# Seven products for eight in the recurrence's projections, with the partial results added in PSUM, and Down's weight sums made by accumulating DMAs

## The chip, the cores and the metric

The kernel runs on one core of one Trainium2 chip. The core has TensorE (PE in the profile: matrix products, results into PSUM), VectorE (DVE), ScalarE (ACT), GpSimd (POOL) and SyncE (SP, which here only issues DMAs). SBUF is the core's working memory, with 128 partitions; PSUM holds eight banks of 512 float32 columns for each partition. The metric is device time in microseconds, the median of some runs.

## The reference

A trunk of two layers over 1024 tokens of width 1024, batch 1. The first layer mixes tokens with a gated linear recurrence of 8 heads of width 128. Its input projection gives four parts, and these projections are what the change touches:

```
q, f, i, g = split(h @ w_in, 4)              # w_in: 1024 x 4096
fg = lb + (1 - lb) * sigmoid(f)
o  = hgrn2_chunkwise(silu(q), 1 - fg, i, log(fg))
o  = o * rsqrt(mean(o^2) + eps) * gnorm_w * silu(g)
mix = o @ w_out
```

`hgrn2_chunkwise` evaluates `S_t = diag(f_t) S_{t-1} + k_t v_t^T`, `o_t = S_t^T q_t`, with k = 1 - fg and v = i. The second layer uses sliding-window attention. After each mixer come a layer norm, a gated feed-forward block (Up: 1024 to 2 x 2816 columns, a causal convolution of width 3, a SiLU gate; Down: 2816 to 1024) and another layer norm. All of it is float32.

## The kernel before, in words

**Precision.** A float32 matrix is split into a high part (rounded to float32r by an ACT copy) and a low part (the rest, by a DVE subtraction). `mm3` (lines 193 to 197) multiplies with three matmuls: high x high, high x low, low x high.

**Residents.** `T` holds the turned activations (channels on partitions), high and low. `Y` is a row buffer of 32 KB a partition. `HL` holds six pairs of high and low weight pieces of 1024 columns.

**Recurrence.** For each head, `qf` computes the query and forget projections with weights as the fixed operand: two halves of 512 tokens, 8 pieces of the contraction, three matmuls each. `ig_block` (L739, L740) computes value and gate with the tokens fixed: 8 blocks of 128 tokens, 8 pieces, and per piece one matmul of 512 columns (high and low weights side by side) and one of 256. `recur` then runs the head's own chain on DVE, PE and ACT, in steps that a generator yields; the heads follow one another in one task, `all_heads`. `norm` normalises, and turns the result back into T, by way of Y for heads 0 to 6. Seven heads' products run beside the previous head's chain.

**Order.** In the recurrence the order on all five engines is written out: the class `Order` counts PE's time (`t`) and DVE's (`v`) as instructions are laid, and steps each generator whose due time has come at every `tick`; `finish` and loops that call `step` run a generator to its end at once. In the feed-forward part only PE's order is written out; the Tile framework orders the others. Each engine's queue runs in order: an instruction that waits holds up those behind it.

**Down's weights.** Down already works with seven products of half blocks for eight, and needs sums of its weight blocks. `slot_begin` (L1193 and around) loads pairs of weight rows into free rows of Y during the recurrence, lays four DVE subtractions each (L1209), 88 for both layers, and stores the sums to the DRAM tile `bsd`, from which `operands` (L562) loads them in Down.

**Up** works with seven products too: `collect` (L477 to L490) adds the products into SBUF on DVE and ACT, and the convolution (L496, L498) follows. Here nothing of that changes.

**The seam.** After the last head the output projection `out_pass` (L1299) and `out_part` use T; `out_proj` loads the residual x into Y (L330), adds the product to it (L351) and starts the layer norms. The second half of the projection's weights comes through `out_late` (rx tiles, L164).

Of the kernel before, what the change touches and what calls it, by code (L numbers as in the profile page):

```python
# [16 lines left out]
P = 128  # L17
S = 1024
# [89 lines left out]
def trunk(ctx: ExitStack, tc: tile.TileContext, a: dict, out: bass.AP):  # L108
# [14 lines left out]
    par = cp.tile([P, 17], F32, name="par")  # L123
# [5 lines left out]
    Y = cp.tile([P, 8, D], F32, name="Y")  # L129
# [7 lines left out]
    nc.gpsimd.dma_start(gd1, a["ln_mix_g"])  # L137
    bsd = [drp.tile([P, FF // 256, 2, D], F32, name=f"bsd{l}") for l in range(2)]
# [54 lines left out]
    def mm3(ps, st, mv, start, stop, n=512):  # L193
        nc.tensor.matmul(ps, st(0), mv(0), start=start, stop=False)  # L194
        nc.tensor.matmul(ps, st(0), mv(1), start=False, stop=False)  # L195
        nc.tensor.matmul(ps, st(1), mv(0), start=False, stop=stop)  # L196
        od.t += 3 * n / 2365.0
# [176 lines left out]
    class Up:  # L374
# [131 lines left out]
        def run(self, ready, down):  # L506
# [18 lines left out]
            self.weights(2)  # L525
            for fc in range(2):
# [11 lines left out]
    class Down:  # L538
# [25 lines left out]
        def operands(self, i, k):  # L564
# [10 lines left out]
            elif p == 5:  # L575
# [3 lines left out]
                tt(R[:, 0], R[:, 0], x[:, 0], op=add)  # L579
                x = R  # L580
            elif p == 6:
                self.block_a(x[:, 0], k, 0, 0)
                self.sum_b(R[:, 1], k, 2)
                tt(R[:, 0], R[:, 0], x[:, 0], op=sub)
                x = R
            elif p == 7:
                self.block_a(x[:, 0], k, 1, 1)
                self.sum_b(x[:, 1], k, 3)
                tt(x[:, 0], x[:, 0], R[:, 0], op=sub)
            elif p == 3:  # L590
                self.block_a(x[:, 0], k, 0, 1)
                self.block_b(x[:, 1], k, 1, 1)
                tt(x[:, 0], x[:, 0], R[:, 0], op=sub)
# [16 lines left out]
        def evacuate(self, p, tb, ps, ln):  # L610
            lo, hi = [Y[:, t, :].rearrange("p (h n) -> p h n", h=2) for t in (tb, tb + 4)]
            both = ps.unsqueeze(1).to_broadcast([P, 2, 512])
            if p == 1:
                for y in (lo, hi):
                    nc.vector.scalar_tensor_tensor(y, y, ALPHA, both, op0=ALU.mult, op1=ALU.add)
            elif p in (6, 7):
                tt(hi, hi, both, op=add)
            for y in {2: [lo[:, 0]], 5: [lo[:, 1], hi[:, 1]], 6: [lo[:, 1]], 3: [lo[:, 1]], 4: [hi[:, 0]]}.get(p, []):
                tt(y, y, ps, op=add)
# [58 lines left out]
    with tc.tile_pool(name="t", bufs=1, reuse_waits="tile") as raws, hgrn_pool as hp:  # L678
        raw_tail(raws)

        def ig_load(h, u):
            return load(lambda r: [(r.rearrange("p (k g c) -> p k g c", k=4, g=2)[:, :, g, :],
                                    w_iv[:, 4 * u:4 * u + 4, (2 + g) * D + h * P:(2 + g) * D + (h + 1) * P])
                                   for g in range(2)])

        def ig_split(raw, eng=None):
            return split_raw(raw, eng).rearrange("p h (k c) -> p h k c", k=4)

        def qf_load(h, g):
            c0 = g * D + h * P  # L690
            return load(lambda r: [(r.rearrange("p (k c) -> p k c", k=KC), w_iv[:, :, c0:c0 + P])])

        def qf_split(raw, eng=None):
            return split_raw(raw, eng).rearrange("p h (k c) -> p h k c", k=KC)

        VG = {-1: hp.tile([P, NB, 2, P], F32, name="VG", bufs=2)}
        values_in, soon, gated = [-1], [], {}

        def values(h, tb, ps):

            vg = VG[h][:, tb]
            nc.scalar.copy(vg, ps[:, 256:].rearrange("p (g c) -> p g c", g=2))
            yield 0.9
            nc.vector.tensor_tensor(vg, vg, ps[:, :256].rearrange("p (g c) -> p g c", g=2), op=ALU.add)
            od.vec(0.45)
            if tb == NB - 1:
                values_in[0] = h
            if tb % 2:
                G = VG[h][:, tb - 1:tb + 1, 1, :]
                sg = hp.tile([P, 2, P], F32, name="sg")  # L710
# [6 lines left out]
        def first_values(ps):  # L717

            pv = ps.rearrange("p (t g c) -> p t g c", t=2, g=2)
            vg = VG[0][:, :2]  # L720
# [957 lines left out]
```

## Time and profile before

| | us |
|---|---|
| median of 3 runs | 2129.36 (2128.87 to 2130.18) |
| span of the profiled execution | 2126.5 |
| PE busy | 2116.9 |
| DVE busy | 1765.4 |
| ACT busy | 926.4 |
| POOL busy | 132.7 |

The profiled execution's own whole time is not listed; the median lies 2.9 us above its span. In the profile a line such as `L1209 DVE TENSOR_TENSOR Y<-Y 128x512` names the line of the kernel, the engine, the operation, and the tiles written and read; then come the count, the busy time with the mean of one, and the engine's idle time before it with what ended it. Matmul durations overlap, so distances between starts are the better measure of TensorE.

### The profile page before, as it was taken

Reading aid. Unit: us, or ns where it says so; the run is one execution under the profiler, and the core shown is the slowest. Engines: PE = TensorE matmul, PEld = TensorE weight load, DVE = VectorE, ACT = ScalarE, POOL = GpSimd, SP = SyncE. Lnnn points to the kernel's source line nnn. Section 1 sums busy time; section 2 is a strip of 40 time slices with the busy share of each in tenths; the row PEclk is TensorE's granted clock in tenths of the full one; section 3 lists DMA queues with packets and bytes.
Section 4 is the critical chain, followed back from the end, with each engine's and each line's share of the span. In section 5 each row is a group of like instructions: output and inputs, shape, how many; then the busy total and the mean of one; then the engine's idle time right before and its main releaser. Section 6 shows DMA issues by size and latency. Waiting matters only on the chain.

```text
span 2126.5 us, 32114 instructions
## 1 busy us (share of the span) xinstructions
PE 2116.9 (100%) x12639; PEld 1776.7 (84%) x12639; DVE 1765.4 (83%) x2378; ACT 926.4 (44%) x1491; POOL 132.7 (6%) x150
## 2 busy tenths in 40 slices
PE   9999999999999999999999999999999999999998
PEld 8888888888888888888888888888888888888887
DVE  4777776677999999888977758969999999878986
ACT  4444444452444444444433356743544444444430
POOL 1000000001100000000001113321000000000002
PEclk9999999999999999999999999999999999999999
DMA  6655443205223222238854511042232222249662
GB/s 218 245 210 168 145 131 120 75 30 180 100 83 98 88 90 80 80 99 272 293 183 166 161 31 41 24 149 90 80 105 94 90 89 80 89 147 334 220 207 97
DMA packets 231566, 280.53 MB, mean 132 GB/s; under 512 B 30152, under 2 KB 160376, under 8 KB 228600
## 3 DMA queue, kind: packets, MB, share of 16 engines
q1 hardware_dynamic: 230464, 278.11, 39.4%
q8 instruction: 99, 1.62, 0.3%
q10 hardware_dynamic: 856, 0.37, 0.1%
q14 instruction: 51, 0.42, 0.1%
q0 software_dynamic: 96, 0.02, 0.0%
HBM read 215.51 MB, written 62.94 MB: 131 GB/s over the span
## 4 chain that ended last, share of the span: by engine, by line
PE 99%; DMA 0%; DVE 0%; SPq 0%; issue 0%; DVEq 0%; ACT 0%; ACTq 0%
PE psmm L194 17%; PE psmm L196 17%; PE psmm L195 17%; PE psax L194 10%; PE psax L195 10%; PE psax L196 10%; PE psmm L739 5%; PE psax L200 4%; PE psmm L740 3%; PE psmm L204 1%; PE psmm L200 1%; PE psax L1452 1%; PE psax L204 1%; PE psmm L1299 1%; PE psmm L777 0%; DMA raw<-in_hgrn_w_in_dram 0%
## 5 line engine op out<-in xcount | busy, mean ns | idle before, releaser
L194 PE MATMUL psmm<-T,HL 128*128 128x512 f32 x768 | 303.5, 395 | 0.0
L196 PE MATMUL psmm<-T,HL 128*128 128x512 f32 x768 | 299.4, 390 | 0.0
L195 PE MATMUL psmm<-T,HL 128*128 128x512 f32 x768 | 299.2, 390 | 0.0
L498 DVE SCALAR_TENSOR_TENSOR Y<-Y,cwt 128x1023 f32<-128x1023 f32 (+1 forms) x176 | 224.9, 1281 | 45.3 <-ACT Y L496 43.9
L221 ACT CAST HL<-rx 128x1024 fp32r<-128x1024 f32 (+1 forms) x151 | 150.7, 1007 | 174.4 <-PE psmm L195 30.4
L169 DVE TENSOR_TENSOR HL<-rx,HL 128x1024 fp32r<-128x1024 f32 (+1 forms) x151 | 178.3, 1187 | 16.5 <-ACT HL L221 16.2
L739 PE MATMUL psmm<-HL,T 128*128 128x512 f32 x496 | 176.8, 399 | 0.0
L196 PEld LDWEIGHTS psmm<-T,HL 128*128 128x128 f32 x768 | 144.2, 188 | 30.5
L194 PEld LDWEIGHTS psmm<-T,HL 128*128 128x128 f32 x768 | 144.3, 188 | 29.7 <-issue 0.4
L195 PEld LDWEIGHTS psmm<-T,HL 128*128 128x128 f32 x768 | 144.4, 188 | 28.8 <-issue 0.4
L496 ACT ACTIVATE Y<-Y,cwt 128x1024 f32<-128x1024 f32 x88 | 108.7, 1238 | 101.5 <-DVE Y L485 89.1
L740 PE MATMUL psmm<-HL,T 128*128 128x256 f32 x496 | 138.9, 280 | 0.0
L194 PE MATMUL psax<-T,HL 128*128 128x512 f32 x352 | 137.3, 390 | 0.0
L196 PE MATMUL psax<-T,HL 128*128 128x512 f32 x352 | 137.0, 389 | 0.0
L195 PE MATMUL psax<-T,HL 128*128 128x512 f32 x352 | 137.0, 389 | 0.0
L243 POOL TENSOR_TENSOR rs<-rs,nhalf 128x1 f32<-128x1 f32 x32 | 44.6, 1396 | 1287.0 <-DVE rs L242 1287.0
L739 PEld LDWEIGHTS psmm<-HL,T 128*128 128x128 f32 x496 | 93.1, 188 | 21.0
L740 PEld LDWEIGHTS psmm<-HL,T 128*128 128x128 f32 x496 | 93.7, 189 | 0.4
L221 ACT CAST HT<-rx 128x1024 fp32r<-128x1024 f32 (+1 forms) x37 | 35.5, 961 | 125.6 <-DVE rx L452 76.7
L169 DVE TENSOR_TENSOR HL<-raw,HL 128x1024 fp32r<-128x1024 f32 x51 | 62.0, 1217 | 21.4 <-ACT HL L176 20.2
L196 PEld LDWEIGHTS psax<-T,HL 128*128 128x128 f32 x352 | 66.1, 188 | 13.6
L195 PEld LDWEIGHTS psax<-T,HL 128*128 128x128 f32 x352 | 66.1, 188 | 13.6
(316 smaller groups left out, 5229.5 us busy)
## 6 DMA issues: line engine op xcount, KB each, us to landing
rx<-in_ffn_w_in_dram SPq DMA_DIRECT2D x136, 256.0 KB, 3.2
rx<-gd SPq DMA_DIRECT2D x118, 256.0 KB, 3.8
Y<-in_ffn_w_out_dram SPq DMA_DIRECT2D x44, 512.0 KB, 6.0
bsd<-Y SPq DMA_DIRECT2D x22, 1024.0 KB, 4.8
gd<-Y SPq DMA_DIRECT2D x44, 512.0 KB, 2.6
rx<-in_ffn_w_out_dram SPq DMA_DIRECT2D x54, 256.0 KB, 4.8
R<-bsd SPq DMA_DIRECT2D x44, 256.0 KB, 5.1
Y<-in_ffn_w_in_dram SPq DMA_DIRECT2D x40, 256.0 KB, 2.9
```

What stands on the lines that cost most here:

```text
L169: make = lambda e: e.tensor_tensor(lo, src, hi.bitcast(F32), op=ALU.subtract)
L194: nc.tensor.matmul(ps, st(0), mv(0), start=start, stop=False)
L195: nc.tensor.matmul(ps, st(0), mv(1), start=False, stop=False)
L196: nc.tensor.matmul(ps, st(1), mv(0), start=False, stop=stop)
L200: nc.tensor.matmul(ps, lhsT, rhs, start=start, stop=stop, **kw)
L204: nc.tensor.transpose(ps, src, ident)
L221: nc.scalar.copy(hi, src)
L243: nc.gpsimd.tensor_tensor(rs, rs, nhalf, op=ALU.pow)
L496: nc.scalar.activation(c, u, AF.Identity, bias=cwt[:, l, 3, ci:ci + 1], scale=cwt[:, l, 2, ci:ci + 1])
L498: nc.vector.scalar_tensor_tensor(c[:, sh:], u[:, :S - sh], cwt[:, l, 2 - sh, ci:ci + 1], c[:, sh:], op0=ALU.mult, op1=ALU.add)
L739: nc.tensor.matmul(ps, T[:, 0, kc, ts], w[:, :, kc % 4, :], start=kc == 0, stop=False)
L740: nc.tensor.matmul(ps[:, :256], T[:, 1, kc, ts], w[:, 0, kc % 4, :], start=False, stop=kc == KC - 1)
```

## The change

- **Units.** For heads 1 to 7 the four projections become two units a head: q with f, and i with g. Each is the product of a weight block matrix (2 x 2 blocks: contraction halves by the two parts) with T (2 x 2: contraction halves by token halves), computed with seven products of half size. Product p is 4 contraction pieces x 3 matmuls of 512 columns.
- **Sums of x.** The block sums of the turned x are made once at the start from a staging tile XS (which replaces Y there); three go to HL (`tx`), and one replaces a quarter of T once head 0's second token half has been projected.
- **Weights.** Each unit's blocks are summed on DVE and split (`prepare`, `cast`) into a tile WR, one unit ahead. WR takes the memory of XS.
- **Adding in PSUM.** Products 1, 6, 7 and 4 go on in one bank, 5 and 3 in another; ACT or DVE read the bank between the products that need a partial result.
- **Values** come out with channels on partitions and are turned by eight transposes (`turn_values`). Gates stay turned, and `norm` multiplies them in after its own transposes.
- **Y** is allocated after the recurrence; heads 0 to 5 go by a DRAM tile `yd` into WR's rows.
- **Down's sums** are made from DRAM to DRAM in Up: 16 plain DMAs from SP and 16 accumulating DMAs from POOL for each layer. Signs in Down's operands and evacuations follow.

```
-    Y = cp.tile([P, 8, D], F32, name="Y")
+    yd = drp.tile([P, 6, S], F32, name="yd")
...
+        def sum_blocks(self):
+            n = FF // 256
+            wb = self.w.rearrange("(r k p) (c n) -> r c p k n", r=2, k=n, c=2)
+            t1, t3, t4, t2 = [self.sums[:, :, i, j * 512:(j + 1) * 512] for i in range(2) for j in range(2)]
+            steps = [((t1, wb[0, 0]), (t3, wb[1, 1]), (t2, wb[1, 1]), (t4, wb[1, 0])),
+                     ((t1, wb[0, 1]), (t3, wb[0, 1])), ((t2, t1),), ((t4, t2),)]
+            for i, step in enumerate(steps):
+                for dst, src in step:
+                    for k0, k1 in ((0, 3), (3, 6), (6, 9), (9, n)):
+                        if i:
+                            nc.gpsimd.dma_start(dst[:, k0:k1], src[:, k0:k1], accum_op=add)
+                        else:
+                            nc.sync.dma_start(dst[:, k0:k1], src[:, k0:k1])
+                        yield
...
             for fc in range(2, NF):
                 if fc > 2:
                     self.weights(fc)
+                for _ in range(2):
+                    next(sums, None)
...
-            early = stash(2, idle[:, :S])
+            early = stash(2, qs if h else VT)
...
+        bank = lambda u, p: {1: banks[u % 2 * 2], 5: banks[3], 3: banks[3], 2: banks[1]}.get(p, banks[u % 2 * 2])
+        units = [(kind, h) for h in range(1, NH) for kind in "qv"]
...
+        def cast(u, p, src):
+            w = WR[0][:, row_of(u, p), :]
+            nc.scalar.copy(w[:, :512], src)
+            job(0.8, 0.69, lambda: low_part(w[:, 512:], src, w[:, :512], None), ("lo", u, p))
...
+            if stage == 0:
+                cast(u, 1, b11)
+                cast(u, 3, b22)
+                plus(1, b11, b12)
+                plus(3, b12, b22)
+                plus(2, b22, b11)
+            elif stage == 1:
+                need(("sum", u, 1))
+                cast(u, 5, b11)
...
+            for k in range(4):
+                mm3(ps, lambda j: w[:, 512 * j + P * k:512 * j + P * k + P], lambda j: moving(j, k),
+                    p in (1, 5, 2) and k == 0, k == 3, more=p in (6, 7, 4, 3))
+                od.tick()
+            collect(u, p, ps)
...
+                def sum22():
+                    tt(st["c"][:, 512:], st["c"][:, 512:], banks[3], op=add)
+                    od.vec(0.69)
+                    od.spawn(second(u, 1), 0.8)
...
+        def drive(cond):
+            n = 0
+            while not cond():
+                for t in sorted(od.chains, key=lambda k: k[0]):
+                    if t is not params:
+                        od.step(t)
+                    if cond():
+                        return
+                if jobs:
+                    lay_job()
...
+        def first_unit():
+            while ("x", 5, 3) not in done_jobs:
+                yield 0.2
+            staging.close()
+            pool = ring_pool.enter_context(tc.tile_pool(name="wr", bufs=1, reuse_waits="tile"))
+            WR.append(pool.tile([P, 8, 1024], F32R, name="WR"))
+            for stage in range(5):
+                prepare(0, stage)
+                yield 1.6
+            prepared.append(0)
...
+            drive(lambda: prepared)
+            last = len(units) - 1
+            stages = {1: 0, 5: 1, 7: 2, 2: 3, 4: 4}
+            for u in range(last + 1):
+                order = [(u, p) for p in ((1, 6, 5, 7, 2, 3) if u < last else (1, 6, 2, 7, 5, 4, 3))]
+                if u:
+                    order.insert(1, (u - 1, 4))
+                for v, p in order:
+                    product(v, p)
...
+            drive(lambda: values_done[0] == NH - 1)
+            drive(lambda: all(m[1] is None for m in late_moves))
...
             for tb in range(4, 6):
                 begun.append(ps[:, (tb - 4) * 512:(tb - 3) * 512])
                 out_part(begun[tb], us, tb, range(KC - 1))
-            od.finish(normed)
+            drive(lambda: 7 in turned)
...
+    Y = ctx.enter_context(tc.tile_pool(name="yp", bufs=1, reuse_waits="tile")).tile([P, 8, D], F32, name="Y")
```

More of the change, by code (lines that the diff above doesn't have):

```diff
@@ L689, in qf_load @@
[L689 to L702, printed above, removed]
+        tail["raw"] = [raws.tile([P, 1024], F32, name=f"raw{i}") for i in range(4)]
@@ new lines, in trunk, with flat, load4, column @@
+        soon, normed = [], []
+        def flat(t):
+            return t.rearrange("p c d -> p (c d)")
+        def load4(loads):
+            raw = tail["raw"][ring["raw"] % 4]
+            ring["raw"] += 1
+            for view, src in loads(raw):
+                nc.sync.dma_start(view, src)
+            return raw
+        def column(g, h):
+            c0 = g * D + h * P
+            return load4(lambda r: [(r.rearrange("p (k c) -> p k c", k=KC), w_iv[:, :, c0:c0 + P])])
+        jobs, done_jobs = [], set()
```

666 lines of the change are left out of this document (416 added, 250 removed).

## The prediction

> **What bounds the kernel now.** I read the page's shares and chain first, then who made TensorE wait, then the busy times of single stages, then single rows of TensorE and VectorE (DVE).
>
> ```profile
> span 2126.5 us, 32114 instructions
> PE 2116.9 (100%) x12639; PEld 1776.7 (84%) x12639; DVE 1765.4 (83%) x2378; ACT 926.4 (44%) x1491; POOL 132.7 (6%) x150
> PE 99%; DMA 0%; DVE 0%; SPq 0%; issue 0%; DVEq 0%; ACT 0%; ACTq 0%
> ```
>
> ```profile
> PE psmm L834 <- DVE Y L785: 1.0, 1, 1.0
> PE psmm L777 <- ACT HL L766: 0.4, 1, 0.4
> PE psmm L777 <- DVE HL L757: 0.3, 1, 0.3
> ```
>
> TensorE is the chain that ends last, nearly alone, and all its waits together are 1.7 us. So every TensorE microsecond removed is worth one, as long as no new wait appears, and every new wait costs itself. That is also the danger: the old order has no wait left to hide a new one behind. The next rows (span of the stretch, busy time and count by engine, granted clock, DMA) show six heads of the recurrence and a piece of the first Up.
>
> ```profile
> 106.00:426.00 320.00, 320.00 (x3294) 272.65 (x3293) 225.75 (x418) 143.37 (x324) 12.87 (x14) 1.00 0.42 141
> 690.00:740.00 50.00, 50.00 (x223) 41.40 (x221) 45.74 (x50) 22.85 (x26) 0.00 (x0) 1.00 0.29 94
> ```
>
> In the recurrence DVE is busy 225.75 / 320 = 71% and ScalarE (ACT) 45%. In Up DVE is busy 91% and TensorE still never waits, so a DVE near 90% is not by itself a bound here.
>
> **What the change takes off TensorE.** Matmul durations overlap (pipelined), so I price by start-to-start distances, from two places of the recurrence:
>
> ```profile
> 396.22 0.40 PE L739 MATMUL psmm<-HL,T 128*128 128x512 f32 x1
> 397.98 0.40 PE L194 MATMUL psmm<-T,HL 128*128 128x512 f32 x1
> 398.22 0.40 PE L195 MATMUL psmm<-T,HL 128*128 128x512 f32 x1
> 400.53 0.39 PE L196 MATMUL psmm<-T,HL 128*128 128x512 f32 x1
> ```
>
> ```profile
> 387.79 1.04 PE L204 MATMUL psax<-ident,og 128*128 128x128 f32 x8
> 388.58 0.48 PE L739 MATMUL psmm<-HL,T 128*128 128x512 f32 x1
> ```
>
> From 396.22 to 397.98 lie five pairs (L739 with 512 columns, L740 with 256): 0.352 us a pair. From 398.22 to 400.53 lie ten steps: 0.231 us for a 512-column matmul. Eight transposes take 388.58 - 387.79 = 0.79. In Up the row above gives 50 / 223 = 0.224 for the same shape.
>
> A head now costs 4 x 24 = 96 matmuls for query and forget (22.2 us) and 8 x 8 = 64 pairs for value and gate (22.5), together 44.7. Afterwards it is two units of 7 products x 12 = 168 matmuls, plus eight transposes, since the value now comes out with channels on partitions. That is 38.8 + 0.8 = 39.6 at 0.231, or 37.6 + 0.8 = 38.4 at 0.224. Over seven heads the gain is 36 or 44 us. I take 38, nearer to the rows of the same stage. Head 0 keeps its 96 matmuls and its pairs; the recurrence's own matmuls stay.
>
> **What moves onto DVE and ACT.** The old groups that go, in the six-head stretch (count, busy us, mean ns):
>
> ```profile
> L1209 DVE TENSOR_TENSOR Y<-Y 128x512 f32<-128x512 f32 x60 | 41.1, 690 | 1.1
> L169 DVE TENSOR_TENSOR HL<-raw,HL 128x1024 fp32r<-128x1024 f32 x23 | 28.0, 1217 | 2.9 <-ACT HL L176 2.9
> L704 DVE TENSOR_TENSOR VG<-VG,psmm 128x256 f32<-128x256 f32 x44 | 18.2, 416 | 10.6 <-ACT VG L702 10.6
> L714 DVE TENSOR_TENSOR VG<-VG,sg 128x256 f32<-128x256 f32 x23 | 9.8, 424 | 7.0 <-ACT sg L712 7.0
> L935 DVE TENSOR_TENSOR qs<-qs,psmm 128x512 f32<-128x512 f32 x11 | 7.5, 684 | 1.8 <-ACT qs L932 1.8
> ```
>
> ACT's sizes, from the whole recurrence:
>
> ```profile
> L925 ACT ACTIVATE fg<-psmm 128x512 f32<-128x512 f32 x16 | 9.6, 598 | 25.7 <-PE psmm L196 18.6 <-DVE tot L1020 7.1
> L1083 ACT COPY kd<-psax 128x1024 f32<-128x1024 f32 x8 | 8.1, 1012 | 2.0 <-PE psax L204 2.0
> ```
>
> The beat of the heads comes from two rows that occur once a head (count, min/median/max ns, first and last start):
>
> ```profile
> L1026 DVE TENSOR_TENSOR St<-qs,kp x8: 1216/1218/1218, 61.5 to 431.8; 128x1024 f32<-128x1024 f32 x8
> ```
>
> ```profile
> L1111 DVE TENSOR_TENSOR og<-psax,VG x8: 1223/1224/1225, 100.8 to 473.2; 128x1024 f32<-128x1024 f32 x8
> ```
>
> (431.8 - 61.5) / 7 = 52.9 us a head, so the stretch holds 6.05 heads and DVE does 37.3 us a head. The five groups are 104.6 us, 17.3 a head. New on DVE, per unit: four sums of weight blocks and five low parts of 512 (9 x 0.69) and one low part of 1024 (1.22), 7.4; twice, 14.9. Then five 512-wide results in the query unit, three in the value unit (8 x 0.69 = 5.5) and the gate (1.22): 21.6 in all. The normalisation keeps two 1024-wide operations. DVE: 37.3 - 17.3 + 21.6 = 41.6 us in a head of 52.9 - 38/7 = 47.5 us, 88%. That is under Up's 91%, so I cost its mass at nothing. Without that cover, each us of DVE over 47.5 a head costs 7. ACT gains some 5 us (ten casts and five copies at about 0.6, less the copy to Y) on 143.37 / 6.05 = 23.7: 60%.
>
> What remains are single waits. The tightest is bank 3: product 3 adds onto products 5 and 7, and the sum of these must first be read by DVE after an ACT copy. Between lies product 2 alone, 12 x 0.228 = 2.7 us, against about 0.6 (ACT) + 0.69 (DVE) when both queues are free. A busy DVE queue can add two operations. I take 2 us over the 14 units; bounds 0 and 1 us in each, 14.
>
> **Head 0 to the first unit.** Before, head 1's products filled TensorE while head 0's recurrence began. Now the first unit's weights use memory that the sums of x must leave first. These sums (16), their low parts (16) and the unit's own ten DVE operations run beside head 0's four products, 4 x 24 x 0.231 = 22.2 us from 36.99.
>
> ```profile
> 36.99 0.40 PE L194 MATMUL psmm<-T,HL 128*128 128x512 f32 x1
> ```
>
> ```profile
> 61.54 1.22 DVE L1026 TENSOR_TENSOR St<-qs,kp 128x1024 f32<-128x1024 f32 x1
> 66.46 1.28 DVE L1035 TENSOR_TENSOR kd<-kp,qp 128x512 f32<-128x512 f32 x2
> ```
>
> 32 x 0.69 = 22 us of sums and low parts fill that time, so the unit's stages come at its end, and the planner, told to go on until the unit is prepared, lays head 0's first block of recurrence (61.54 to 67.74, 6.2 us) between them. TensorE ends head 0 at 59.2 and product 1 at 61.9. Product 6 needs the 1024-wide low part, which I put behind that block: about 60.7 + 6.2 + 1.2 = 68.1, a wait of 6. The column sums follow with another 1. I take 7. Bounds: 0 if the low part is laid ahead, 12 if the other low parts go before it too. The preamble gets eight ACT copies of 1 us and some DVE sums: 1 us, 0 to 3.
>
> No wait of TensorE in this trace is over 1.0 us and its clock reads 1.00 throughout the stages above, so no row shows what a long pause does to the clock. The Trainium skill (TensorE: Matmul & The Clock Gate, Part 1: The HAM clock gate) states that about 3.4 us of idleness halve the clock until some 3.4 us of work have passed. By it, as an estimate from that page, a 6 us pause costs 1.7 us more.
>
> **End of the recurrence.** Head 7's recurrence starts about 9 us into the last unit and takes 473.2 - 431.8 = 41.4 us, thus until 50. TensorE has eight products (21.9), 84 passes of the output projection (19), the transposes and about 12 us of recurrence of its own ahead of it: some 54. Covered; but its last transposes are forced behind the blocks of tb 4 and 5, so one DVE, ACT, DVE pass over a quarter (1.4 us) shows. I take 2, 0 to 6.
>
> Then Y. It is now allocated after the recurrence, over the recurrence's tiles:
>
> ```profile
> SPq L330 <- DVE T L169: 35.3, 1, 35.3
> ```
>
> ```profile
> 475.63 3.53 SPq L330 DMA_DIRECT2D Y<-in_x_dram  x7
> 479.26 13.52 SPq L164 DMA_DIRECT2D rx<-in_hgrn_w_out_dram  x8
> ```
>
> ```profile
> 489.79 0.48 DVE L226 SCALAR_TENSOR_TENSOR T<-psax,par,T 128x256 fp32r<-128x256 f32 x1 [0.54 <-ACT T L225]
> 493.69 1.37 DVE L351 SCALAR_TENSOR_TENSOR Y<-Y,psmm 128x512 f32<-128x512 f32 x2 [0.61 <-PE psmm L196]
> ```
>
> The residual loads already waited 35.3 us for the moves out of Y. If Y shares bytes with head 7's gate, they wait until its last split, about 490.3, which is 14.7 us later, and on SP's queue the second half's weights (rx, x8) stand behind them.
>
> ```profile
> 496.89 0.39 PE L194 MATMUL psmm<-HL,T 128*128 128x512 f32 x1
> ```
>
> ```profile
> GB/s 218 245 210 168 145 131 120 75 30 180 100 83 98 88 90 80 80 99 272 293 183 166 161 31 41 24 149 90 80 105 94 90 89 80 89 147 334 220 207 97
> ```
>
> ```profile
> Y<-in_x_dram SPq DMA_DIRECT2D x16, 512.0 KB, 7.9
> ```
>
> At the 334 GB/s of the fastest slice 4.2 MB of Y and 2.1 MB of rx land by 509.2, at 280 by 513; with cast and low part (2.2) the last pair is ready at 511 or 515. TensorE starts the blocks of tb 6 and 7 at 496.89, so it wants these weights from 507.7 and the last pair at 511.8. I take 4; bounds 0 (Y's tiles free early) and 12 (if each Y load takes the 7.9 us of its row).
>
> **Down's sums.** They leave DVE (counted) and SP's queue in the recurrence. In Up come, per layer, 16 plain copies from SP (about 0.8 MB each, two to a column block, in the way of weight loads that are issued a block ahead) and 16 accumulating copies from POOL.
>
> ```profile
> q1 hardware_dynamic: 230464, 278.11, 39.4%
> ```
>
> ```profile
> bsd<-Y SPq DMA_DIRECT2D x22, 1024.0 KB, 4.8
> Y<-in_ffn_w_out_dram SPq DMA_DIRECT2D x44, 512.0 KB, 6.0
> ```
>
> ```profile
> L562 SPq DMA_DIRECT2D R<-bsd x44: 319/384/1461, 998.1 to 1979.6; - x44
> ```
>
> ```profile
> L477 ACT COPY Y<-psmm x24: 584/591/607, 574.9 to 1893.4; 128x512 f32<-128x512 f32 x24
> ```
>
> The queue's packets take 0.394 x 16 x 2126.5 / 230464 = 58 ns for 1.2 KB on average. 5632 rows of 2 KB at about 100 ns on 16 engines are 35 us of copying, and as much or twice that for the sums, in some 400 us at DMA share 0.29. No row shows an accumulating DMA. Nearest: a load and a store of that size, 6 + 6 + 4.8, so up to 17 us each. Up's fifth product ends at 574.9, so block 2 begins near 574.9 + 9 x 2.7 = 599 and the sixteen are laid from block 10 on, near 599 + 8 x 18.9 = 750; the first is read at 998: 248 us, 15.5 each. POOL does nothing there (0.00 in the Up row) and DMAs overlap, so 0 is nearer than 16 x 1.5 = 24 a layer. Above 15.5 serial us each the excess counts sixteen times per layer (d). Evacuations in Down change in sign and are cut in 512s: under 1 us a layer, behind a TensorE that does not wait.
>
> **The sum.** -38 + 7 + 1 + 2 + 2 + 4 = -22 on the span of 2126.5: 2104.5. The median of the runs, 2129.36, lies 2.9 above that span; with it 2107. All bounds good give 2129 - 44 = 2085, all bad, but for Down, 2129 - 36 + 12 + 3 + 14 + 6 + 12 = 2140.
>
> **Rivals.** (a) The waits are all but hidden by the planner, as now: 2085 (all bounds good) to 2094. For it: the old order has none. Against: the old order never had to force a chain forward before it could go on. 0.08.
> (b) The accumulation in PSUM brings its own waits: product 3 waits for DVE's reading of bank 3 in each unit, 1.5 us. 14 x 1.5 = 21 more, 2122 to 2133 with the bounds of the seams. For it: 88% DVE in one queue, with reads placed between operations that wait for TensorE; against: Up reads seven products a block at 91% without a wait. 0.13.
> (c) Slower: the recurrence's own chain becomes the bound. Heads run one after another, each at 39 to 41 us (rows L1026, L1111) in a beat that shrinks to 47.5, and 21.6 us of DVE work for the units stand in the same queue where 17.3 stood. It decides from 47.5 + 22/7 = 50.6 us a head; at 55 us it costs 7 x (55 - 50.6) = 31 over 2129, 2160. Against: the chain has 6 us of room. 0.12.
> (d) Slower: the sums are not ready when Down reads them. At 25 us each, 16 x 9.5 x 2 = 304 late, 2411. For it: no accumulating DMA has run in this trace. 0.05. The Trainium skill (DMA: Bandwidth & Descriptors, SWDGE vs HWDGE vs iDMA) adds that accumulation is generated in software by GpSimd only, which VectorE can lock out of its port; no run so far shows it.
>
> **Chances.** Forecast 0.62, its own range 2094 to 2122. Less than 0.2% (4.3 us) from 2129.4 can't be told from no change. Faster: 0.62 + 0.08 + 0.04 of (b) = 0.74. Same: 0.07 of (b). Slower: 0.12 + 0.05 + 0.02 of (b) = 0.19. The range, 2092 to 2132, leaves out most of (a), (c) and (d).
>
> **What would show it.** Right: TensorE's waits appear after 59 us and around 490 to 512 and nowhere else, once-a-head rows stand 47 to 48 us apart, Up and Down keep their length. Wrong: a beat above 50; waits of TensorE for DVE at each third product; TensorE waiting for DMA in Down; waits at the seam of 10 us and more, where Y's loads start later than the last split.

## The result, and the profile after

The changed kernel takes 2370.36 us (median of 4 runs, 2368.49 to 2372.26) against 2129.3 before: a ratio of 1.1133, with a 95% interval of 1.1117 to 1.1149. It is 241 us slower, and the forecast of 2107 with its range of 2092 to 2132 was wrong. The page of the changed kernel (span, busy times, TensorE's busy tenths and granted clock in 40 slices, shares of the chain that ended last):

```profile
span 2367.6 us, 31570 instructions
...
PE 2115.7 (89%) x12303; PEld 1754.2 (74%) x12303; DVE 1801.3 (76%) x2445; ACT 973.8 (41%) x1556; POOL 173.4 (7%) x182
...
PE   9630068999897999999999999999999999999998
...
PEclk9865579999998999999999999999999999999999
...
PE 81%; issue 10%; DVE 5%; ACT 2%; POOL 2%; DMA 1%; DVEq 0%; POOLq 0%; SPq 0%; ACTq 0%
```

A slice is 59 us. TensorE, which waited 1.7 us in all before, stands still in two of them, at 180 to 300 us, and its granted clock reads 0.5 there; from the fourteenth slice on, in Up, Down and the second layer, both rows are full again. TensorE's busy time is the same as before although 336 matmuls are gone. Who made TensorE wait, the three longest:

```profile
PE psax L204 <- DVE og L1199: 161.3, 1, 161.3
PE psax L200 <- ACT kd L1155: 18.6, 1, 18.6
PE psmm L196 <- DVE WR L169: 8.8, 3, 3.3
```

One wait of 161.3 us, for the normalised output of head 0 (og). VectorE's own longest wait:

```profile
DVE og L1195 <- POOL ss L1192: 154.4, 2, 149.8
```

It stood 149.8 us for ss, which GpSimd makes. GpSimd's timeline at the end of the hole, and all sums of Down's weights by kind (count, min/median/max ns, first and last start):

```profile
302.68 1.23 POOL L561 DMA_DIRECT2D bsd<-bsd  x1 [6.36 <-issue]
310.40 1.15 POOL L561 DMA_DIRECT2D bsd<-bsd  x1 [6.50 <-issue]
311.63 0.19 POOL L1191 TENSOR_SCALAR ss<-ss 128x8 f32<-128x8 f32 x1
311.90 1.69 POOL L1192 TENSOR_TENSOR ss<-ss,nhalf 128x8 f32<-128x8 f32 x1
```

```profile
L563 SPq DMA_DIRECT2D bsd<-in_ffn_w_out_dram x32: 609/1959/12972, 19.5 to 125.2; - x32
L561 POOL DMA_DIRECT2D bsd<-in_ffn_w_out_dram x16: 1136/1228/1352, 28.5 to 250.6; - x16
L561 POOL DMA_DIRECT2D bsd<-bsd x16: 1140/1227/1242, 135.8 to 310.4; - x16
```

All 64 DMAs of both layers, which the code lays between Up's products, were issued between 19.5 and 310.4 us, in the recurrence. Head 0's two small GpSimd operations stand in the queue behind the last of the 32 accumulating DMAs, which follow one another at some 7.7 us here (302.68 to 310.40). The cause is in the order of the queues: in the feed-forward part only TensorE's order is written out. A DMA from one DRAM tensor to another depends on no product, so nothing ties it to Up, and the framework put all of them ahead. The raw weight loads of the projections stood behind the plain copies on SP's queue as well, here two of them behind 19 copies that take 53.35 us:

```profile
58.86 53.35 SPq L563 DMA_DIRECT2D bsd<-in_ffn_w_out_dram  x19
112.32 12.80 SPq L718 DMA_DIRECT2D raw<-in_hgrn_w_in_dram  x2
```

### The profile page after: what moved, and what is told of

Same layout as the page of the kernel before. It is cut to its first block, busy times and chain, and to the rows that moved or that the text cites. A ratio compares the mean times of both kernels' runs of the same rounds, so it can differ in the third digit from the quotient of the medians.

```text
span 2367.6 us, 31570 instructions
## 1 busy us (share of the span) xinstructions
PE 2115.7 (89%) x12303; PEld 1754.2 (74%) x12303; DVE 1801.3 (76%) x2445; ACT 973.8 (41%) x1556; POOL 173.4 (7%) x182
## 4 chain that ended last, share of the span: by engine, by line
PE 81%; issue 10%; DVE 5%; ACT 2%; POOL 2%; DMA 1%; DVEq 0%; POOLq 0%; SPq 0%; ACTq 0%
PE psmm L194 15%; PE psmm L196 15%; PE psmm L195 15%; PE psax L194 9%; PE psax L195 9%; PE psax L196 9%; PE psax L200 3%; POOL bsd L561 1%; PE psmm L204 1%; PE psax L204 1%; PE psmm L200 1%; PE psax L1719 1%; DMA raw<-in_hgrn_w_in_dram 1%; PE psmm L1553 1%; DVE qp L1086 0%
## 5 line engine op out<-in xcount | busy, mean ns | idle before, releaser
L194 PE MATMUL psmm<-T,HL 128*128 128x512 f32 x512 | 200.6, 392 | 0.0
L196 PE MATMUL psmm<-T,HL 128*128 128x512 f32 x512 | 199.3, 389 | 0.0
L195 PE MATMUL psmm<-T,HL 128*128 128x512 f32 x512 | 199.3, 389 | 0.0
L204 PE MATMUL psax<-ident,og 128*128 128x128 f32 x64 | 10.1, 311 | 167.4 <-DVE og L1199 161.3
L496 ACT ACTIVATE Y<-Y,cwt 128x1024 f32<-128x1024 f32 x88 | 108.7, 1238 | 101.5 <-DVE Y L485 89.1
L204 PEld LDWEIGHTS psax<-ident,og 128*128 128x128 f32 x64 | 8.7, 161 | 168.8 <-DVE og L1199 161.5
L1195 DVE TENSOR_TENSOR og<-psax,ss 128x1024 f32<-128x1024 f32 x8 | 9.7, 1218 | 154.4 <-POOL ss L1192 154.4
L196 PEld LDWEIGHTS psmm<-T,HL 128*128 128x128 f32 x512 | 96.0, 187 | 20.2
L194 PEld LDWEIGHTS psmm<-T,HL 128*128 128x128 f32 x512 | 96.2, 188 | 19.7
L195 PEld LDWEIGHTS psmm<-T,HL 128*128 128x128 f32 x512 | 96.2, 188 | 19.3
L194 PE MATMUL psmm<-T,WR 128*128 128x512 f32 x224 | 91.8, 410 | 0.0
L195 PE MATMUL psmm<-T,WR 128*128 128x512 f32 x224 | 89.4, 399 | 0.0
L196 PE MATMUL psmm<-T,WR 128*128 128x512 f32 x224 | 89.2, 398 | 0.0
L194 PE MATMUL psmm<-HL,WR 128*128 128x512 f32 x168 | 69.3, 413 | 14.2 <-ACT fg L1306 4.9
```

Source lines behind the costliest of these rows:

```text
L194: nc.tensor.matmul(ps, st(0), mv(0), start=start, stop=False, skip_group_check=more)
L195: nc.tensor.matmul(ps, st(0), mv(1), start=False, stop=False, skip_group_check=more)
L196: nc.tensor.matmul(ps, st(1), mv(0), start=False, stop=stop, skip_group_check=more)
L204: nc.tensor.transpose(ps, src, ident)
L496: nc.scalar.activation(c, u, AF.Identity, bias=cwt[:, l, 3, ci:ci + 1], scale=cwt[:, l, 2, ci:ci + 1])
```

## The experiments

**Down's part alone.** The old kernel with the change's class Down and its use in Up; the recurrence lays no weight sums any more:

```
-        free, units, loaded, summed = {r: 0 for r in (0, 2, 4, 6)}, list(range(2 * pairs)), [], []
+        free, units, loaded, summed = {r: 0 for r in (0, 2, 4, 6)}, [], [], []
```

> The kernel before, with Down's sums by DMA as in the change and nothing else of it (old projections, old Y, no sums on VectorE). Theory Q: the 32 accumulating DMAs stand ahead of the first norm on GpSimd's queue as they do in the changed kernel; the first head's transposes, at about 119 us, wait until about 314: 2129 + 195 = about 2325. Theory D: slower too, but with waits spread over Up or Down. Theory P: near 2129.

It took 2333.4 us (one run). All but 1 us of TensorE's waiting is again one wait of the same kind:

```profile
PE psax L204 <- DVE og L1146: 201.7, 1, 201.7
```

So the sums alone, with the old projections, make the hole.

**The sums held back until Up.** In the changed kernel, and in the old kernel with Down's part, a DMA of 16 numbers from a row of Y that the running block of Up has written goes into each quarter of bsd before its first copies. The order follows from data; the work is the same.

```
+    if not i:
+        mark = Y[0:1, 4 + block() % 2, 0:16].rearrange("p (a b) -> p a b", a=4)
+        nc.sync.dma_start(dst[0:1, 0::3, 0:4], mark)
```

> The changed kernel, with one small DMA (16 numbers from Y, just made by Up) written into each quarter of bsd ahead of its first copies, four per layer, so that no sum can go ahead of Up in any queue. Theory Q (the queues' order costs the time: the sums have nothing to wait for, so they stand ahead of the recurrence's own work on GpSimd's and SyncE's queues): the 161 us wait goes and the time falls by about 200 to 235 us, to 2135 to 2170; TensorE's waits inside heads 2 to 7 (24 us in the changed kernel) and at the seam (14 us) stay. Theory D (the accumulating DMAs cost by themselves, wherever they run): over 2200, with TensorE waits in Up or Down. Theory P (the seven-product projections cost the time): near 2370.

> The kernel before, with Down's sums by DMA, tied to Up by small DMAs: the second part of the change alone, in the place that its text shows. Theory Q: 2125 to 2133, as TensorE has no wait that the freed VectorE could shorten. Theory D: over 2180.

The changed kernel took 2213.7 us (2210.95 to 2216.05), ratio 1.0398 (1.0383 to 1.0414); the old one with Down's part 2140.8, ratio 1.0055 (1.0038 to 1.0072). The place in the queues is worth 157 us, and the sums in Up, with the small DMAs that hold them back, still cost 12 us. But 85 us of loss remained, twice the most that I had expected.

**The projections alone.** The sums are left out of the computation, and Down reads plain blocks in their place:

```
-            sums = down.sum_blocks()
+            sums = iter(())
...
-            nc.sync.dma_start(dst, self.sums[:, k, i, j * 512:(j + 1) * 512])
+            self.block_b(dst, k, i, j)
```

> The changed kernel without any of the 64 DMAs of the sums; Down reads the plain weight blocks where it would read the sums, so what Down computes with them is left out, its work stays. Theory Q: within 5 us of the kernel with the sums tied to Up, since 7.7 us each on an idle GpSimd queue is hidden. Theory D: at least 50 us below it. Theory P: near 2370.

It took 2199.2 us (2197.79 to 2199.88), ratio 1.033 (1.0314 to 1.0345). The projections that I had put at -22 cost +70. Its busy times, TensorE's two longest waits, and two rows of TensorE from the start:

```profile
PE 2114.4 (96%) x12303; PEld 1753.3 (80%) x12303; DVE 1800.6 (82%) x2445; ACT 973.5 (44%) x1556; POOL 135.2 (6%) x150
```

```profile
PE psax L204 <- DVE og L1199: 11.5, 1, 11.5
PE psmm L196 <- DVE WR L169: 8.9, 3, 3.3
```

```profile
67.32 0.64 PE L200 MATMUL psax<-St,one 128*32 128x256 f32 x8 [3.15 <-DVE St L1097]
...
84.15 0.80 PE L194 MATMUL psmm<-T,WR 128*128 128x512 f32 x1
```

The span less the busy time is 83 us of standing still, against 9.6 before. At the start, head 0's column sums and first blocks of scores are written ahead of the first unit's first product, at 84.15, and TensorE waits at them one after another. The code shows why. Where a tile must be free before the order can go on, `drive` steps every chain once, whether it is due or not, together with one VectorE job, until its condition holds:

```
        while not cond():
            for t in sorted(od.chains, key=lambda k: k[0]):
                if t is not params:
                    od.step(t)
                ...
```

**Steps by due time.** The same work, but in `drive` one chain at a time is stepped, the one due first, and the planner's clock moves up to it:

```
-                for t in sorted(od.chains, key=lambda k: k[0]):
-                    if t is not params:
-                        od.step(t)
-                    if cond():
-                        return
-                if jobs:
+                t = min([c for c in od.chains if c is not params], key=lambda k: k[0])
+                if jobs and jobs[0][0] <= t[0]:
+                    od.t = max(od.t, jobs[0][0])
                     lay_job()
+                else:
+                    od.t = max(od.t, t[0])
+                    od.step(t)
```

> The changed kernel without Down's sums (2199.2 us), but where the order must free a tile before it goes on (drive), the chains are stepped one at a time by their due times and the planner's clock is moved up to them, instead of one step of every chain and one VectorE job in turn. The work is the same. In the kernel without this edit drive put steps up to 16.8 us ahead of their due times: head 0's column sums ahead of the first unit, and the normalisations of heads 0 and 1 15.2 and 10.0 us early. Theory F (forced steps: TensorE waits in its written order for work put too early): the start's waits (some 13 us between 64 and 84) and those for og (11.5 and 6.1 us) go, and with them most of the low clock before 240 us: 2150 to 2175. Theory M (VectorE's mass is the bound, 41.6 us a head): the same work, so 2199 within 8 us. Theory A (ScalarE's in-order queue: casts stand behind copies that wait for VectorE): some 2190 to 2205.

2156.2 us (2154.3 to 2156.81), ratio 1.0127 (1.0112 to 1.0142): 43 us less for an order alone, as expected. Its busy times, and its stretches (span; busy and count of PE, PEld, DVE, ACT, POOL; clock, DMA share, GB/s):

```profile
PE 2105.4 (98%) x12303; PEld 1746.9 (81%) x12303; DVE 1803.1 (84%) x2445; ACT 974.4 (45%) x1556; POOL 132.8 (6%) x150
```

```profile
65.00:120.00 55.00, 41.30 (x440) 33.34 (x441) 38.83 (x70) 25.98 (x56) 1.23 (x2) 0.81 0.07 20
120.00:442.90 322.90, 315.78 (x3106) 257.16 (x3105) 248.75 (x428) 173.18 (x354) 12.55 (x13) 1.00 0.17 53
...
500.00:570.00 70.00, 55.48 (x227) 44.04 (x227) 54.25 (x81) 18.36 (x25) 5.04 (x4) 0.88 0.46 165
```

Between 120 and 443 us TensorE stands still for 7.1 us only. What is left of the loss lies at the two ends.

**VectorE's mass.** The four sums of weight blocks per unit (56 operations of 0.69 us, 38.6 us) are left out of the computation, once with the forced steps and once with steps by due time:

```
-            plus = lambda key, x, y: job(0.0, 0.69, lambda: tt(x, x, y, op=add), ("sum", u, key))
+            plus = lambda key, x, y: job(0.0, 0.0, lambda: None, ("sum", u, key))
```

> The changed kernel without Down's sums (2199.2 us) and also without the four sums of weight blocks in each unit (56 VectorE operations of 0.69 us, 38.6 us over the recurrence; left out of the computation). Theory M (VectorE's mass): each us of VectorE over the beat is worth one: 2199 - 38 = 2161 (2155 to 2175). Theory F (forced steps): the order of TensorE is the same but for the planner's VectorE clock, so 2190 to 2200. Theory A (ScalarE's queue): the two casts a unit that wait for a sum wait no more, 2185 to 2195.

> The run with steps by due time (2156.2 us), and without the four sums of weight blocks in each unit (38.6 us of VectorE, left out of the computation). Without them the kernel with forced steps fell by 37.7 us, which the theory of forced steps had not foreseen. Theory F2 (VectorE's work counts only as lateness of the recurrence, which the forced steps then turn into TensorE waits; with steps by due time TensorE stands still only 7 us between 120 and 443 us): 2148 to 2156. Theory M (VectorE's mass is worth its time whatever the order): 2156 - 38 = 2118, not above 2130.

With forced steps it took 2161.5 us, 37.7 less, which I had not expected of the forced steps and had named as the sign of a VectorE that is the bound. With steps by due time it took 2150.7, only 5.5 less for the same 38.6 us. The second pair is the clean one. With steps by due time, 2428 of the recurrence's 2436 TensorE operations beside the units keep their place among the units' matmuls (within three of them) when the sums are left out. With forced steps 924 of the 2436 move (the edit also has the planner count these jobs at 0). So VectorE's mass by itself is worth a seventh of its time. How much of the 37.7 us is mass that the forced order turned into TensorE waits, and how much is the other order, no run separates. The stretch of 240 to 420 us with forced steps, all work in place first, then without the sums:

```profile
240.00:420.00 180.00, 166.91 (x1646) 136.82 (x1645) 130.69 (x227) 94.41 (x203) 9.29 (x8) 1.00 0.15 45
```

```profile
240.00:420.00 180.00, 178.52 (x1881) 146.08 (x1880) 126.91 (x224) 96.28 (x195) 5.50 (x6) 1.00 0.16 48
```

VectorE does almost as much in both (130.69 and 126.91); TensorE gets 11.6 us more done in the second.

**ScalarE's queue.** The casts of weight blocks on GpSimd:

```
-            nc.scalar.copy(w[:, :512], src)
+            nc.gpsimd.tensor_copy(w[:, :512], src)
```

> The changed kernel without Down's sums (2199.2 us), with the units' casts of weight blocks (70 copies of 512 and 14 of 1024 columns) on GpSimd, idle in the recurrence, instead of ScalarE. Theory A (a cast stands behind a copy of ScalarE that waits for VectorE, and the low part behind the cast): the waits for low parts (8.9 us), for fg and for the gates (8.8) go, with the cold clock behind them: 2175 to 2185. Theory F: these waits alone move, 2188 to 2200. Theory M: no change, or slower where GpSimd's copy takes longer than 0.62 us.

2219.5 us (2218.44 to 2220.49), 20 us slower than with the casts on ScalarE. The waits for low parts stayed (8.8 us). The same VectorE operation in the run without and with casts on GpSimd, 120 to 480 us:

```profile
L1086 DVE TENSOR_TENSOR qp<-qp,tot 128x512 f32<-128x512 f32 x36 | 24.7, 686 | 22.0 <-PE psax L200 22.0
```

```profile
L1086 DVE TENSOR_TENSOR qp<-qp,tot 128x512 f32<-128x512 f32 x36 | 27.5, 763 | 25.7 <-PE psax L200 25.7
```

The casts took 0.868 us in the mean and 0.608 at best, where ScalarE's took 0.62, and this VectorE operation became 11% longer in the mean. The run therefore does not clear ScalarE's queue by itself; it shows only that this way out is closed.

**A buffer for product 1.** On top of the steps by due time, product 1's result goes to a tile of its own instead of into qs:

```
-                    drive(lambda: queries_done[0] >= h - 1)
-                    state[u]["q"] = hp.tile([P, S], F32, name="qs")
+                    state[u]["c11"] = hp.tile([P, S // 2], F32, name="c11")
...
+                if kind == "q":
+                    drive(lambda: queries_done[0] >= h - 1)
+                    st["q"] = hp.tile([P, S], F32, name="qs")
```

To make room, the same edit shrinks the tile `one` and lets some small setup tiles share memory with others.

> As the run with steps by due time, and product 1's result goes to a buffer of its own (512 columns) instead of into qs, so that a query unit need not wait for the recurrence of the head before to have read qs until its product 2. Theory F with the handover of qs as its cause (by the planner's own clock the recurrence's end comes at 405 instead of 422 us): 10 to 20 us below the run with steps by due time, thus 2135 to 2160. If qs is not what binds: the same as that run within 4 us.

A miss: 2190.2 us, 34 more than without the buffer. TensorE's longest waits between 120 and 540 us are new ones:

```profile
PE psmm L194 <- ACT fg L1305: 12.7, 4, 3.8
PE psmm L196 <- DVE WR L169: 9.6, 2, 4.8
```

The planner's clock had 17 us less for this order. It counts TensorE and VectorE, not ScalarE; these waits lead to ScalarE's copies and casts. That the missing count is the cause is likely, but no run here shows it, and none takes the buffer apart from the shared small tiles.

**The two ends.** At the start, 36 matmuls that compute nothing needed fill TensorE's longest pause; at the end, four tiles that are free early are put where Y will lie:

```
+            for _ in range(36):
+                nc.tensor.matmul(banks[3], T[:, 0, 0, :P], T[:, 0, 0, :512], start=True, stop=True)
...
+        for n in ("qs", "fg", "kd", "kp"):
+            hp.tile([P, S], F32, name=n)
         VG = hp.tile([P, 2, NB, P], F32, name="VG")
```

> The run with steps by due time, with 36 matmuls of 128x512 (8.4 us) that compute nothing needed put where TensorE waits 9.0 us for the first unit's weights; they go to a bank that is free until the unit's third product. Theory C (a pause costs twice: itself, and a slow clock after it): the 0.81 of 65 to 120 us rises, and of the 55 x 0.19 = 10.5 us lost to it 4 to 9 come back: 2147 to 2152. Rival: the low clock is spread over the many small pauses of that stretch, or comes from something other than the pause: 2155 to 2157.

> The run with steps by due time, with four tiles of the recurrence (qs, fg, kd, kp) given the memory right behind the raw weights, so that Y, which is allocated over the first 32 KB of the recurrence's memory, lies over tiles that are free some 25 us before head 7's gate. Theory Y (Y's residual loads wait for the last split of head 7's gate, 504.2 to 504.7 us, and rx behind them): the loads start near 480, TensorE's waits of 4.6 us (Y L351), 2.4 (TX) and part of 6.6 (Y L255) go with the low clock of 0.88 behind them: 2140 to 2150. Rival (the end of the recurrence itself holds the seam, its chain of normalisation, transposes and splits): 2153 to 2157.

The filler changed nothing: 2156.3 us. Rows of TensorE without it, and with it:

```profile
72.54 0.80 PE L194 MATMUL psmm<-T,WR 128*128 128x512 f32 x1 [9.03 <-ACT WR L1238]
81.45 1.06 PE L200 MATMUL psax<-VT 128*32 128x16 f32 x64 [2.21 <-ACT VT L1074]
```

```profile
71.49 0.50 PE L194 MATMUL psmm<-T,WR 128*128 128x512 f32 x1 [0.87 <-ACT WR L1238]
80.39 1.05 PE L200 MATMUL psax<-VT 128*32 128x16 f32 x64 [4.35 <-ACT VT L1074]
```

The first unit's first product took less with a warm clock, and the next wait grew from 2.21 to 4.35 us. In this stretch head 0's chain sets the pace (VectorE is busy 21.61 of the 25 us from 65 to 90), so the slow clock fell into time that was lost anyway. Y over early tiles took 2149.1 us (2148.79 to 2149.16), 7 less: the residual loads start 25.8 us sooner, without and with the edit:

```profile
504.72 4.37 SPq L330 DMA_DIRECT2D Y<-in_x_dram  x8
```

```profile
478.89 3.76 SPq L330 DMA_DIRECT2D Y<-in_x_dram  x8
```

TensorE's wait for Y at L351 fell from 4.6 to 0.5 us; those for TX (2.4) and for Y at L255 (6) stayed, so something else holds them. The rival's chain of splits and norms is likely; no run singled it out.

**The whole computation, and what the sums cost in Up.** With both mends and the sums, marks and copies first on GpSimd's queue, then on SP's with marks read from a stored block of gd; and the latter on the old kernel. The first run's edit, and that of the other two:

```
-                        nc.sync.dma_start(dst[0:1, 0::3, 0:4], mark)
+                        nc.gpsimd.dma_start(dst[0:1, 0::3, 0:4], mark)
...
-                            nc.sync.dma_start(dst[:, k0:k1], src[:, k0:k1])
+                            nc.gpsimd.dma_start(dst[:, k0:k1], src[:, k0:k1])
```

```
-    mark = Y[0:1, 4 + block() % 2, 0:16].rearrange("p (a b) -> p a b", a=4)
+    mark = gd[0:1, block() - 2, 0:16].rearrange("p (a b) -> p a b", a=4)
```

> The whole computation again: the changed kernel with steps by due time and Y over tiles that are free early (2149.1 us without Down's sums), and Down's sums held back until Up by the 16 numbers from Y, but with these marks and the plain copies on GpSimd's queue instead of SP's. On SP's queue the marks cost the old kernel 11.4 us: one wait of TensorE early in each Up (3.9 and 3.2 us, Y L483) and a slow clock after it, while SP's queue stood at a mark for 5.7 us with weight loads behind it. Theory S (SP's queue standing at a mark makes the Up weights late; the sums themselves cost nothing there, as the prediction had it): 2148 to 2153. Rival D (the DMA traffic of the sums, 0.8 to 0.97 of the engines in that stretch, makes the weights late whichever queue issues it): 2157 to 2165. If GpSimd's queue makes the sums late for Down: above 2170, with TensorE waits for bsd in Down.

> The whole computation: the changed kernel with steps by due time, Y over tiles that are free early (2149.1 us without Down's sums) and the sums held back until Up by marks that are read from a block of gd in DRAM, stored two blocks before, and issued with the copies from SP's queue. Theory S2 (the cost so far was that of the marks): 2149 to 2154, no wait over 1 us in Up. Rival D (DMA traffic or the eight copies in front of weight loads cost by themselves): 2157 to 2165, with the waits of 3 to 4 us early in each Up that the marks from Y had.

> The old kernel with Down's part of the change alone, marks as in the run above (2140.8 us with marks from Y). Theory S2: 2128 to 2132, thus the prediction's 0 for the sums in Up holds once they stand there. Rival D: 2138 to 2143.

They took 2207.9, 2175.6 (ratio 1.0217, 1.0202 to 1.0232) and 2152.7 us (1.01, 1.0083 to 1.0117). On GpSimd's queue a mark stands behind slow sums, and ScalarE's next write of that row of Y must wait until the mark has read it. The rows of GpSimd, ScalarE and VectorE show it: the mark at 726.19, ScalarE's wait of 19.49 us for it, and VectorE's wait for ScalarE's L496 that ends at 733.42:

```profile
726.19 0.97 POOL L563 DMA_DIRECT2D bsd<-Y  x1
732.42 1.52 POOL L568 DMA_DIRECT2D bsd<-in_ffn_w_out_dram  x2 [5.27 <-DMA bsd<-Y]
```

```profile
732.15 1.24 ACT L496 ACTIVATE Y<-Y,cwt 128x1024 f32<-128x1024 f32 x1 [19.49 <-DMA bsd<-Y]
733.42 1.28 DVE L498 SCALAR_TENSOR_TENSOR Y<-Y,cwt 128x1023 f32<-128x1023 f32 x1 [18.91 <-ACT Y L496]
```

With marks from gd that trouble is gone, and sums and marks together still cost 26.5 us on the mended kernel and 23.4 on the old one. Both lie above what either theory had given, and in the old kernel above the 12 us with marks from Y. But these marks are not free either. In the old kernel SP's queue, which also carries the weight loads, stood for the store of gd that a mark reads, and then for the marks to land:

```profile
SPq L563 <- DMA gd<-Y: 34.5, 6, 7.9
SPq L568 <- DMA bsd<-gd: 25.2, 8, 4.5
```

That is 59.7 us of standing over both layers, against 30.9 with marks from Y. So these runs do not show how much the sums cost without any marks. SP's time to issue one of Up's weight loads between 560 and 800 us (min/median/max ns), in the old kernel and in the old one with these sums, and a stretch of each:

```profile
L441 SPq DMA_DIRECT2D rx<-in_ffn_w_in_dram x42: 367/409/573, 563.9 to 789.5; - x42
```

```profile
L441 SPq DMA_DIRECT2D rx<-in_ffn_w_in_dram x40: 367/506/7687, 563.9 to 787.6; - x40
```

```profile
650.00:700.00 50.00, 50.00 (x222) 41.42 (x221) 48.16 (x55) 23.59 (x27) 0.00 (x0) 1.00 0.34 105
```

```profile
650.00:700.00 50.00, 44.84 (x188) 36.56 (x187) 42.04 (x49) 17.89 (x21) 5.95 (x5) 0.93 0.90 210
```

The DMA engines are busy at 0.90 there (0.34 in the old kernel), a load's issue takes up to 7.7 us (0.573 at most in the old kernel), and TensorE loses 5 us in these 50. Whether sums spread singly over the whole of Up would cost nothing was not tried. No version beat the old kernel; the best whole one with the new projections, 2175.6, is 46 us behind it.

## Why the prediction was wrong

**The step that failed first** is the one on Down's sums: "the sixteen are laid from block 10 on, near 599 + 8 x 18.9 = 750", and so 0. It took the place in the code for the place in the queue. That is 157 of the 241 us. My rival (d) came near in time (2411), but by luck, since its mechanism was the opposite: the sums were not late for Down, they were early, in front of the recurrence. "POOL does nothing there" was looked up for Up, not for where the DMAs went. And held in Up they are not free either: 12 to 26 us, marks included. Taken away one after another, the parts of the 241 us are 157 for the place in the queues, 15 for the sums and marks in Up, 43 for the forced steps, and 27 that stay with steps by due time.

**The terms of the sum**, on the run with steps by due time, whose span is 28.5 us above the old one. Its TensorE is busy 2105.4 us, of which the slow clock is 41.30 x 0.19 + 55.48 x 0.12 = 14.5; so the removed work is 2116.9 - 2090.9 = 26 us, not 38. This is an estimate: the mean clock of a stretch also covers time in which TensorE stands still, and counted on the rows at half speed alone the slow clock is some 11 us and the removed work 23. The term was right in kind and mis-sized: I priced the units' matmuls at 0.231 us, the spacing inside a run of them. Between 180 and 420 us, 752 of them take 185.6 us from start to start, of which 4.6 are waits: 0.241. Counted in the same way from 106 to 426 us, the old query and forget matmuls stood at 0.237 (562 in 133.0 us) and the old pairs at 0.353. With these prices the gain is 7 x (96 x 0.237 + 64 x 0.353 - 168 x 0.241 - 0.8) = 28 us, so the spacing explains most of the difference.

| term | forecast | measured |
|---|---|---|
| TensorE's work | -38 | -26 (23 to 28) |
| before head 0's chain (37 to 65) | +1 | +3 |
| head 0 to the first unit (65 to 120) | +7 | 13.7 still, 7.8 slow clock |
| waits in the units (120 to 443) | +2 | +7 |
| end and seam (500 to 570) | +6 | 14.5 still, 6.7 slow clock |

The last column adds to 27, next to 28.5; the slow clock stands in it twice with opposite signs, so its size does not matter to the sum. The gap at the start was twice its size, with a cause that was read rightly in part. VectorE does lay head 0's first block of recurrence there, from 64.97 to 71.1 us, but ahead of the last low part of T and not only of the 1024-wide one of the weights:

```profile
71.11 0.69 DVE L169 TENSOR_TENSOR T<-XS,T 128x512 fp32r<-128x512 f32 x1
71.87 1.14 ACT L1238 CAST WR<-raw 128x512 fp32r<-128x512 f32 x2 [7.73 <-DVE T L169]
```

WR takes the memory of XS, so its first cast waits for that last reading of XS, and the 9.03 us fall on product 1, not on product 6. The waits that follow in head 0's chain (2.21 and 1.39 us) and for qs (2.55), and the slow clock, were not in the term. At the seam the bytes that Y shares were read rightly and cost 7 us; the wait at L255 was not in the sum.

**The beat.** I took 52.9 us a head from the first and last of the once-a-head rows. Two neighbouring rows from the middle of the stage, of the old kernel and of the run with steps by due time:

```profile
158.64 1.22 DVE L1026 TENSOR_TENSOR St<-qs,kp 128x1024 f32<-128x1024 f32 x1
214.77 1.22 DVE L1026 TENSOR_TENSOR St<-qs,kp 128x1024 f32<-128x1024 f32 x1
```

```profile
228.87 1.22 DVE L1097 TENSOR_TENSOR St<-qs,kp 128x1024 f32<-128x1024 f32 x1
282.04 1.22 DVE L1097 TENSOR_TENSOR St<-qs,kp 128x1024 f32<-128x1024 f32 x1
```

56.1 went to 53.2, not 52.9 to 47.5. The old beats are not steady: the seven run from 45.8 to 56.2 us, and the mean over them lies below what TensorE's work of one head takes, 45.3 us of projections by the prices above and some 11 of the recurrence's own matmuls. By the same mean from first to last row the new beat is 54.0, longer than 52.9. VectorE's load was read rightly: 248.75 us from 120 to 443 us, six beats, is some 41 a head, where I had 41.6.

**The rest**, 43 us between the forced order and the one by due time, is a loss that no term held. Rival (b), product 3 waiting at bank 3, is there but small: in the run with steps by due time the waits for L1312, which reads that bank, add to 6 us over 14 units, 0.4 us each in place of 1.5. Rival (c), the chain as the bound, came near in size, since its rule gives 2129 + 7 x (59.0 - 50.6) = 2188 for the mean beat of 59.0 with forced steps, and 2199.2 was measured. But the chain is not the bound: in due order the beat is 53.2 with TensorE busy 98% of 120 to 443 us. "The old order never had to force a chain forward" stood in the text as the argument against rival (a) only; it was the argument for a loss.

**The clock.** The traces now show what a pause does: after 9.03 us the next matmuls stand 0.43 us apart, not 0.23, for some 4.9 us. The sentence from the Trainium skill (TensorE: Matmul & The Clock Gate, Part 1: The HAM clock gate), half clock for some 3.4 us of work, agrees with the rate, while the stretch was longer here, 4.9 us. But the filler shows that counting it on top of a wait, as that estimate would, is not safe either: where another engine sets the pace, a slow TensorE costs nothing.

## What to carry to other kernels

Where a framework orders the queues, ask of each moved DMA what data it waits for: if nothing, its line in the code said nothing here about its place in the queue, and it belongs in the sum of the stage to which the queue can pull it. An order that is forced forward to free a tile should be followed by its due times, chain by chain, before any engine's mass is counted. And a mean beat taken from the first and the last row should be checked against two neighbours.

## What the runs showed of the hardware

An accumulating DMA from DRAM to DRAM of 768 KB held GpSimd's queue for 7.7 us from one to the next (1.2 us of it its own instruction, 6.4 before it without a wait that the profile shows). The last 24, of 512 and 768 KB, started 7.6 us apart in the mean, from 135.84 to 310.40 us, with the DMA engines busy at 0.64. The Trainium skill (DMA: Bandwidth & Descriptors, SWDGE vs HWDGE vs iDMA) names one such queue, fed by GpSimd alone, and the traces agree. GpSimd's casts and VectorE's operations were both slower side by side (casts of 0.868 us in the mean, 0.608 at best; VectorE's L1086 0.763 us where it took 0.686); the Trainium skill (SBUF — State Buffer, SBUF: two separate sides) has the two engines share a port that one of them holds for a whole instruction, which agrees in kind.
